# Wider spacing of a ring of weight tiles in a 1-core transformer trunk

## Chip, cores and metric

The kernel runs on one core of one Trainium2 chip. The metric is the time of one execution on the device, in microseconds (us). Before the change it is 2625.57 us, the median of three runs from 2624.16 to 2627.06 us.

## What is computed

Two layers, each a token mixer and a gated feed-forward network, over 1024 tokens of 1024 features in float32. Layer 0 mixes with forgetting attention (8 heads of 128), layer 1 with chunked retention (4 heads, chunks of 64 tokens). Cut to what matters:

```python
def rmsnorm(x, g):
    return x * rsqrt(mean(x * x, -1) + 1e-6) * g

def forgetting_attention(h, w_in, b_f, w_out):        # w_in: 1024 x (3*1024 + 8)
    q, k, v, f = split(h @ w_in)
    c = cumsum(log_sigmoid(f + b_f), axis=1)          # one decay per token and head
    s = q @ k.T * 128 ** -0.5 + (c[query] - c[key])   # causal
    return softmax(s) @ v @ w_out

def retention(h, w_in, w_out):                        # w_in: 1024 x 6144
    q, k, v, g = split(h @ w_in); q, k = rotate(q), rotate(k) / 16
    # per chunk: inner products with decay, a state carried from chunk to chunk
    return (silu(g) * normalised(y)) @ w_out          # w_out: 2048 x 1024

def swiglu(h, w_in, w_out):                           # 2816 hidden features
    gu = h @ w_in
    return (silu(gu[:2816]) * gu[2816:]) @ w_out

x = x + forgetting_attention(rmsnorm(x)); x = x + swiglu(rmsnorm(x))
x = x + retention(rmsnorm(x));            x = x + swiglu(rmsnorm(x))
out = rmsnorm(x)
```

## The kernel before

Activations stay in feature-major tiles of 128 partitions by 512 tokens. Every operand of a product is an exact sum of two float32r parts, a high part and a low part. `split` (L97 to L99) makes them: ScalarE casts the source into the high tile (L98), VectorE subtracts it from the source into the low tile (L99). A product of two such operands takes three matmuls: high by high, high weight by low activation, low weight by high activation (L106 to L108 in `mm_u`, L638 to L640 in `Products`). Each matmul loads its own 128x128 block of weights and streams 512 columns of activations past it.

The large products of the feed-forward and the retention projections are Strassen-Winograd products in 2 x 2 blocks, seven in place of eight. `Blocks` loads a pair of weight tiles into `st`, forms their sums on VectorE (`s1`, `s2`) and splits each on demand; `Products` runs 12 matmuls for each of the seven: four 128-column slices of one split weight tile, three matmuls a slice. A few products (`pair_N`, L737 to L739, and `v_pair`, L256 to L258) use the split weight tile as the streamed operand in place of the loaded one.

All split weights go through one ring, made in `wh_wl` (L79 and L80) from the pool `wp`: six tiles with tag `wh` for high parts and six with tag `wl` for low parts. A tile holds 512 float32r values per partition and 16 spare ones, 2112 bytes in all. The split activations are tiles with tag `b` of exactly 2048 bytes, in the pools `bpa` (ahead of the ring in memory) and, after the attention stage, `bpb` (behind it).

In the built program the first `wh` slot starts at byte 107008 of each partition (a multiple of 256) and the slots follow at the pitch of 2112 bytes; the six `wl` slots come right behind them, from byte 119680. So the starting byte, modulo 256, is 0, 64, 128, 192, 0, 64 for the six `wh` slots and 128, 192, 0, 64, 128, 192 for the six `wl` slots. The four slices of a tile lie 512 bytes apart and have the tile's own residue. All `b` tiles start at multiples of 256. A slot is given to the tile that asks next when its last reader is done, so high and low slots come in all pairings.

In the attention stage (a pool `fox` that is released before the Strassen stages) `attend` (L313) ends each block of 512 queries with the reciprocal of the denominator in a tile `rec` and the block's output in a tile `o`, one buffer each (L379 to L398): two ScalarE activations (L383, L384) and two VectorE instructions (L385, L386) make the reciprocal, L387 multiplies it into `o`, and `split` reads `o`. `decay_bias` (L269) keeps its 128x64 intermediates in small tiles; `f_s` is read last at L289 and `f_lf` is written at L292.

The order of the instructions on each engine comes from the framework's scheduler.

Of the kernel before, what the change touches and what calls it, by code (L numbers as in the profile page):

```python
# [17 lines left out]
P = 128  # L18
# [19 lines left out]
def trunk(ctx, tc, nc, d, out):  # L38
# [22 lines left out]

# [1 line left out]
    bpa = ctx.enter_context(tc.tile_pool(name="bpa", bufs=32))  # L63
# [15 lines left out]
    def wh_wl(width=512):  # L79
        return [wp.tile([P, 512 + 16], F32R, tag=t, name=nm(t))[:, :width] for t in ("wh", "wl")]  # L80

# [29 lines left out]

# [1 line left out]
    class Norm:  # L113
# [69 lines left out]

    # =================== forgetting attention ===================
    with ExitStack() as fs:
# [6 lines left out]
        def half(tag, bufs=2):  # L192
            if tag in ("t", "x"):
                return yp.tile([P, H], F32, tag="y", name=nm(tag))
            return fp.tile([P, H], F32, tag=tag, name=nm(tag), bufs={"rec": 1, "o": 1}.get(tag, bufs))

# [72 lines left out]
        def decay_bias(z):  # L269
            n = TB * FOX_HEADS  # L270
            zz = z.rearrange("p b h -> p (b h)")
            m = small([P, n], "f_m", 1)
            sg = small([P, n], "f_sg", 1)
            s = small([P, n], "f_s", 1)
            s2 = small([P, n], "f_s2", 1)
            a = small([P, n], "f_a", 1)
            nc.vector.tensor_scalar(m, zz, -1.0, None, op0=ALU.mult)
            nc.vector.tensor_tensor(m, m, zz, op=ALU.min)
            sig = nc.scalar.activation(sg, m, AF.Sigmoid)
            with tc.issue_after(sig.ins):  # L280
                nc.scalar.preload_act_table_set("natural_log_exp_and_others")
            nc.vector.tensor_scalar(s2, sg, -1.0, 2.0, op0=ALU.mult, op1=ALU.add)
            nc.vector.reciprocal(s2, s2)
            nc.vector.tensor_tensor(s, sg, s2, op=ALU.mult)
            nc.vector.tensor_tensor(s2, s, s, op=ALU.mult)
            nc.vector.tensor_scalar(a, s2, 1.0 / 19.0, None, op0=ALU.mult)
            for j in range(8, 0, -1):
                nc.vector.scalar_tensor_tensor(a, a, 1.0 / (2 * j + 1), s2, op0=ALU.add, op1=ALU.mult)
            nc.vector.scalar_tensor_tensor(a, a, 1.0, s, op0=ALU.add, op1=ALU.mult)  # L289
            nc.vector.tensor_scalar(m, zz, 0.0, None, op0=ALU.min)  # L290
            lf = small([P, n], "f_lf", 1)
            nc.vector.scalar_tensor_tensor(lf, a, -2.0, m, op0=ALU.mult, op1=ALU.add)  # L292
            ps = mp.tile([P, H], F32, tag="ms", name=nm("c"))
            nc.tensor.matmul(ps[:, 0:n], tri, lf, start=True, stop=True)
            nc.tensor.matmul(ps[:, n:2 * n], ones, lf, start=True, stop=True)
            pre = small([P, TB + 1, FOX_HEADS], "f_pre", 1)
            nc.vector.memset(pre[:, 0, :], 0.0)
            for b in range(TB):
                nc.vector.tensor_tensor(pre[:, b + 1, :], pre[:, b, :],
                                        ps[:, n + b * FOX_HEADS:n + (b + 1) * FOX_HEADS], op=ALU.add)  # L300
            c = small([P, TB, FOX_HEADS], "f_c", 1)
            nc.vector.tensor_tensor(c, ps[:, 0:n].rearrange("p (b h) -> p b h", b=TB), pre[:, 0:TB, :], op=ALU.add)
            dk = []
            for qh in range(2):
                t = small([P, TB, FOX_HEADS], f"f_d{qh}", 1)
                nc.vector.tensor_tensor(t, pre[:, 4 * qh + 2:4 * qh + 3, :].to_broadcast([P, TB, FOX_HEADS]), c,
                                        op=ALU.subtract)
                dk.append(t)
            return dk
# [3 lines left out]
        def attend(h, kk, qq, vs, dk, rks):  # L313
# [4 lines left out]
            def weights(qb):  # L318
# [57 lines left out]
                else:  # L376
                    den = mp.tile([P, H], F32, tag="ms", name=nm("den"))
                    nc.tensor.matmul(den, ones, acc, start=True, stop=True)
                rec, o = half("rec"), half("o")  # L379
                n = 2 if h == FOX_HEADS - 1 and qb else 1  # L380
                for cs in (slice(i * H // n, (i + 1) * H // n) for i in range(n)):
# [4 lines left out]
                    nc.vector.scalar_tensor_tensor(r, sm[:, cs], 2.0, r, op0=ALU.subtract, op1=ALU.mult)  # L386
                    nc.vector.scalar_tensor_tensor(o[:, cs], pv[:, cs], -1.0, r, op0=ALU.mult, op1=ALU.mult)  # L387
                if h >= FOX_HEADS - 2:
# [4 lines left out]
                    for cs in (slice(i * H // n, (i + 1) * H // n) for i in range(n)):  # L393
                        split(hi[:, cs], lo[:, cs], o[:, cs])
                    return
                oh = fp.tile([P, H], F32R, tag="ph", name=nm("oh"), bufs=3)
                ol = fp.tile([P, H], F32R, tag="pl", name=nm("ol"), bufs=3)
                split(oh, ol, o)  # L398
                nc.sync.dma_start(od[h][0][:, HALF[qb]], oh.bitcast(F32))
# [15 lines left out]
        reloads = []  # L415
        # the keys of the first two heads, a pass over the features as they come
        ks, pss = [], {}
# [27 lines left out]
        for h in range(FOX_HEADS):  # L445
# [6 lines left out]
            if h == FOX_HEADS - 1:  # L452
# [1 line left out]
                wo, ops = [], {}  # L454
# [7 lines left out]

        # the tiles so far with all heads but the last; the first of them leave the banks
        part = {}
# [15 lines left out]

    # =================== Strassen-Winograd products ===================
    # C = A B with A = W^T in 2 x 2 blocks (two column tiles, even and odd k tiles) and
    # B in 2 x 2 blocks (even and odd k tiles, two token halves): seven products.
    bpb = ctx.enter_context(tc.tile_pool(name="bpb", bufs=24))
# [10 lines left out]

    # where the sums of a phase are kept
    NAMES = ("B11", "T2", "T1", "T3", "B21", "B22", "T4")
# [40 lines left out]
    class Stored:  # L538
        """The sums of a group of four pairs of feature tiles, kept in memory, split at their first use."""

# [28 lines left out]
    class Blocks:  # L569
        """The four blocks of a pair of column tiles and their sums, split on demand."""  # L570

# [46 lines left out]
    class Products:  # L618
        """The seven products of one pair of 128-column tiles, feature-major."""

# [21 lines left out]
    def pair_acc(src, X, y, first):  # L642
        """Adds the products of one pair to the sums y over the groups of feature tiles."""
        prod = Products(src, X)
# [25 lines left out]
    def paired_out(wsrc, stored, scale_rows, xold):  # L670
        """x + (scaled) act @ W over the groups of eight feature tiles whose sums are in memory."""
        ys = [{} for _ in range(4)]
# [20 lines left out]
    def pair_T(src, X):  # L693
        """Feature-major C11, C12, C21, C22 of one pair of 128-column tiles."""
        prod = Products(src, X)
# [20 lines left out]
    def pair_N(srcs, X):  # L716
        """Token-major C11, C12, C21, C22 of one pair of 256-column tiles, as two tiles of two token blocks."""
        ws = [Blocks(s) for s in srcs]
# [58 lines left out]
    def load_units(pool, src, gate=None):  # L777
        """A feature tile over all tokens from memory, split in two, by token halves."""
        r = []
# [10 lines left out]
    def out_proj(wsrc, y, acts, xnew, gi, nextw, pools):  # L790
        """y + act @ W: returns the operands of the next phase and its norm."""
        norm = Norm(gi, sp, "sc", "sacc", 4)
# [17 lines left out]

    # =================== SwiGLU ===================
    def ffn(i, X, nrm, xold, xnew, last, nw, pools):
# [60 lines left out]

# [1 line left out]
    norm = Norm(1, sp, "sc", "sacc", 4)  # L875
# [34 lines left out]

    # =================== retention ===================
    qd = [[dp.tile([P, S], F32, tag=f"qd{k}", name=f"qd{k}") for k in range(2 * h, 2 * h + 2)] for h in range(RET_HEADS)]
# [81 lines left out]
    def load_k(h):  # L994
        """Keys by feature, split, and the first half of them times kappa by token, split."""
        ks, kf = [], []
# [23 lines left out]
    def state(kt, vv):  # L1020
        """Sum over the first half of the tokens of key times value, by key feature."""
        r = []
# [146 lines left out]
def _alt(w, i):  # L1169
    """Every other column tile."""  # L1170
    k, n = w.shape
    return w.reshape(k, n // 256, 2, P)[:, :, i].reshape(k, n // 2)


def _quad(u, v, js):
    """A pair of column tiles as four blocks: the first over even and over odd k tiles, then the second."""
    r = [w.reshape(KT // 2, 2, P, -1)[list(js)].transpose(2, 1, 0, 3).reshape(P, 2, -1) for w in (u, v)]
# [76 lines left out]
```

## Time and profile before

| | |
|---|---|
| time, median of three runs | 2625.57 us |
| span of the profiled execution | 2626.0 us |
| TensorE (PE) busy | 2600.0 us, 99% |
| weight loads (PEld) busy | 2179.9 us, 83% |
| VectorE (DVE) busy | 1960.2 us, 75% |
| ScalarE (ACT) busy | 1155.9 us, 44% |
| GpSimd (POOL) busy | 167.6 us, 6% |
| granted TensorE clock, mean | 0.998 of full speed |

The profile gives the profiled execution's own time as this span, from its first to its last instruction. Matmuls overlap in the pipeline, so the duration of one (394 ns) is longer than the distance from its start to the start of the next; what the stream costs is that distance, called the pitch below. A window of the profile that holds N matmuls without a break in T us has a pitch of T/N.

### The profile page before, as it was taken

The numbers are of one execution on the slowest core, as the hardware profiler recorded it, in microseconds if no ns is written. First come the engines' busy times: TensorE is split into PE (matmuls) and PEld (weight loads), VectorE is DVE, ScalarE is ACT, GpSimd is POOL, SyncE is SP. The second block draws the span as 40 slices with busy tenths as digits, with TensorE's granted clock in tenths as the row PEclk, the third lists the DMA queues.
The fourth block names the chain that finished last, engine by engine and source line by source line (L and its number), as shares of the span: only waits on it lengthen the run. The fifth ranks groups of instructions, "written<-read, shape, count | busy, mean of one in ns | idle before, by whom it ended". The sixth has DMA issues, their size and how long they took to land.

```text
span 2626.0 us, 35148 instructions
## 1 busy us (share of the span) xinstructions
PE 2600.0 (99%) x12808; PEld 2179.9 (83%) x12808; DVE 1960.2 (75%) x3367; ACT 1155.9 (44%) x2168; POOL 167.6 (6%) x147
## 2 busy tenths in 40 slices
PE   9999999999999999999999999999999999999998
PEld 8878887888888878889898989898888888887888
DVE  6798888877767778987667676885567776768795
ACT  6566666533233444453333425662353233335533
POOL 0143322000000000001000010000000000000000
PEclk9999999999999999999999999999999999999999
DMA  3111143332332345533332325655522332325441
GB/s 129 44 57 65 49 145 119 122 106 95 109 104 97 109 152 180 167 107 117 104 113 96 113 101 160 189 196 192 190 85 85 104 111 86 109 84 183 156 158 65
DMA packets 137694, 312.11 MB, mean 119 GB/s; under 512 B 15665, under 2 KB 28721, under 8 KB 137521
## 3 DMA queue, kind: packets, MB, share of 16 engines
q1 hardware_dynamic: 136800, 309.33, 35.1%
q8 instruction: 100, 1.64, 0.3%
q14 instruction: 74, 0.60, 0.1%
q10 hardware_dynamic: 720, 0.55, 0.1%
HBM read 217.54 MB, written 92.27 MB: 118 GB/s over the span
## 4 chain that ended last, share of the span: by engine, by line
PE 89%; DMA 4%; DVE 3%; issue 2%; ACT 1%; POOL 0%; SPq 0%; DVEq 0%; POOLq 0%; ACTq 0%
PE mm L638 17%; PE mm L640 17%; PE mm L639 17%; PE mm L106 7%; PE mm L107 7%; PE mm L108 7%; PE mm L738 2%; PE mm L739 2%; PE mm L737 2%; DMA st<-vd 1%; DMA st<-ac_T 1%; PE mm L256 1%; PE mm L258 1%; PE mm L257 1%; DVE b L99 1%
## 5 line engine op out<-in xcount | busy, mean ns | idle before, releaser
L639 PE MATMUL mm<-b,wh 128*128 128x512 f32 x2128 | 836.8, 394 | 0.0
L638 PE MATMUL mm<-b,wh 128*128 128x512 f32 x2128 | 832.9, 395 | 3.2 <-ACT 22_4397_22190 L653 1.8
L640 PE MATMUL mm<-b,wl 128*128 128x512 f32 x2128 | 819.5, 394 | 0.1
L98 ACT CAST wh<-st 128x512 fp32r<-128x512 f32 (+1 forms) x449 | 275.2, 616 | 578.4 <-PE mm L639 409.4
L638 PEld LDWEIGHTS mm<-b,wh 128*128 128x128 f32 x2128 | 400.3, 188 | 97.8 <-ACT 22_4397_22190 L653 2.2
L640 PEld LDWEIGHTS mm<-b,wl 128*128 128x128 f32 x2128 | 399.8, 188 | 94.1 <-DVE wl L99 0.9
L639 PEld LDWEIGHTS mm<-b,wh 128*128 128x128 f32 x2128 | 400.0, 188 | 91.9 <-DVE b L99 0.2
L99 DVE TENSOR_TENSOR wl<-st,wh 128x512 fp32r<-128x512 f32 (+1 forms) x449 | 311.5, 697 | 55.8 <-ACT wh L98 51.8
L98 ACT CAST wh<-s 128x512 fp32r<-128x512 f32 x252 | 156.0, 621 | 413.3 <-PE mm L639 356.8
L106 PE MATMUL mm<-b,wh 128*128 128x512 f32 x736 | 289.7, 397 | 8.4 <-ACT b L126 5.7
L107 PE MATMUL mm<-b,wh 128*128 128x512 f32 x736 | 290.0, 395 | 1.4 <-DVE b L99 1.4
L108 PE MATMUL mm<-b,wl 128*128 128x512 f32 x736 | 289.9, 395 | 0.0
L99 DVE TENSOR_TENSOR wl<-s,wh 128x512 fp32r<-128x512 f32 x252 | 182.6, 727 | 41.4 <-ACT wh L98 39.7
L106 PEld LDWEIGHTS mm<-b,wh 128*128 128x128 f32 x736 | 138.9, 189 | 40.5 <-ACT b L126 6.5
L107 PEld LDWEIGHTS mm<-b,wh 128*128 128x128 f32 x736 | 138.8, 189 | 32.0 <-DVE b L99 1.8
L108 PEld LDWEIGHTS mm<-b,wl 128*128 128x128 f32 x736 | 138.7, 188 | 31.5
L98 ACT CAST b<-st 128x512 fp32r<-128x512 f32 (+1 forms) x216 | 125.1, 612 | 81.7 <-DMA st<-ac_T 30.0
L99 DVE TENSOR_TENSOR b<-st,b 128x512 fp32r<-128x512 f32 (+1 forms) x216 | 140.0, 674 | 27.9 <-ACT b L98 22.5
L711 DVE TENSOR_TENSOR u<-mm,u 128x512 f32<-128x512 f32 x60 | 41.4, 689 | 116.1 <-PE mm L640 115.9
L738 PE MATMUL mm<-wl,b 128*128 128x256 f32 x448 | 126.0, 281 | 0.0
L739 PE MATMUL mm<-wh,b 128*128 128x256 f32 x448 | 125.9, 281 | 0.0
L737 PE MATMUL mm<-wh,b 128*128 128x256 f32 x448 | 125.8, 281 | 0.0
(514 smaller groups left out, 3965.2 us busy)
## 6 DMA issues: line engine op xcount, KB each, us to landing
st<-ffn_in SPq DMA_DIRECT2D x88, 512.0 KB, 3.5
st<-ffn_out_pairs SPq DMA_DIRECT2D x32, 512.0 KB, 5.4
st<-ac_T SPq DMA_DIRECT2D x32, 512.0 KB, 4.6
ac_T<-t SPq DMA_DIRECT2D x48, 256.0 KB, 2.4
st<-ac_B SPq DMA_DIRECT2D x24, 512.0 KB, 4.6
st<-fox_qk SPq DMA_DIRECT2D x32, 256.0 KB, 2.7
xo<-xd SPq DMA_DIRECT2D x32, 256.0 KB, 3.1
ac_B<-p SPq DMA_DIRECT2D x32, 256.0 KB, 3.1
```

The source lines that it names most:

```text
L98: nc.scalar.copy(hi, src)
L99: return nc.vector.tensor_tensor(lo, src, hi.bitcast(F32), op=ALU.subtract)
L106: nc.tensor.matmul(ps, wh, xh, start=(first and k == 0), stop=False)
L107: nc.tensor.matmul(ps, wh, xl, start=False, stop=False)
L108: nc.tensor.matmul(ps, wl, xh, start=False, stop=(last and k == n - 1))
L638: nc.tensor.matmul(ps, hi[:, js], th, start=f, stop=False, skip_group_check=not new)
L639: nc.tensor.matmul(ps, hi[:, js], tl, start=False, stop=False, skip_group_check=not new)
L640: nc.tensor.matmul(ps, lo[:, js], th, start=False, stop=(j == 3), skip_group_check=not new)
L711: nc.vector.tensor_tensor(u2, banks["c"], u2, op=ALU.add)
L737: nc.tensor.matmul(o, th[:, tk], hi[:, js], start=f, stop=False, skip_group_check=sk)
L738: nc.tensor.matmul(o, th[:, tk], lo[:, js], start=False, stop=False, skip_group_check=sk)
L739: nc.tensor.matmul(o, tl[:, tk], hi[:, js], start=False, stop=(j == 3), skip_group_check=sk)
```

## The change

Each tile of the ring gets 64 spare values in place of 16: 2304 bytes in place of 2112. Twelve tiles of 192 bytes more are 2304 bytes per partition. They come from two tiles of the attention stage that go: `o` (2048 bytes), whose value is now written over `rec`, and `f_lf` (256 bytes), which becomes a second use of `f_s`.

```diff
     def wh_wl(width=512):
-        return [wp.tile([P, 512 + 16], F32R, tag=t, name=nm(t))[:, :width] for t in ("wh", "wl")]
+        return [wp.tile([P, 512 + 64], F32R, tag=t, name=nm(t))[:, :width] for t in ("wh", "wl")]
...
-            return fp.tile([P, H], F32, tag=tag, name=nm(tag), bufs={"rec": 1, "o": 1}.get(tag, bufs))
+            return fp.tile([P, H], F32, tag=tag, name=nm(tag), bufs={"rec": 1}.get(tag, bufs))
...
-            lf = small([P, n], "f_lf", 1)
+            lf = small([P, n], "f_s", 1)
...
-                rec, o = half("rec"), half("o")
+                rec = half("rec")
...
-                    nc.vector.scalar_tensor_tensor(o[:, cs], pv[:, cs], -1.0, r, op0=ALU.mult, op1=ALU.mult)
+                    nc.vector.scalar_tensor_tensor(r, pv[:, cs], -1.0, r, op0=ALU.mult, op1=ALU.mult)
...
-                        split(hi[:, cs], lo[:, cs], o[:, cs])
+                        split(hi[:, cs], lo[:, cs], rec[:, cs])
...
-                split(oh, ol, o)
+                split(oh, ol, rec)
```

The other lines of the diff only remove comments. Apart from the new names, the instructions of every engine stand in the same order in the built program as before. Three ScalarE instructions have another list of waits: the first activation of L383 in two of the 16 blocks of queries now also waits for VectorE (the last reader of the shared tile in the block before), and one cast of L98 no longer does.

In the built program the `wh` slots start at byte 107008 as before and follow at 2304 bytes, the `wl` slots start at byte 120832. 2304 is nine times 256, so all twelve start at multiples of 256, alternately at 0 and 256 modulo 512. What lies behind the ring moves up by 2304 bytes or, behind a removed tile, by less; every one of the `b` tiles still starts at a multiple of 256.

## Rows read from the trace of the kernel before

**Rows 1.** Page, part 1: busy us (share of the span) and instructions, by engine.

```profile
PE 2600.0 (99%) x12808; PEld 2179.9 (83%) x12808; DVE 1960.2 (75%) x3367; ACT 1155.9 (44%) x2168; POOL 167.6 (6%) x147
```

**Rows 2.** Windows of two feed-forward stages: busy us and (instructions) by engine, clock, DMA.

```profile
530.00:925.00 395.00, 395.00 (x1706) 320.42 (x1705) 284.98 (x459) 130.57 (x222) 0.00 (x0) 1.00 0.31 107
2100.00:2365.00 265.00, 265.00 (x1146) 215.18 (x1145) 187.11 (x302) 82.07 (x139) 0.00 (x0) 1.00 0.29 97
```

**Rows 3.** Page, part 5, matmul groups: shapes, count | busy, mean ns | idle before.

```profile
L639 PE MATMUL mm<-b,wh 128*128 128x512 f32 x2128 | 836.8, 394 | 0.0
...
L107 PE MATMUL mm<-b,wh 128*128 128x512 f32 x736 | 290.0, 395 | 1.4 <-DVE b L99 1.4
...
L738 PE MATMUL mm<-wl,b 128*128 128x256 f32 x448 | 126.0, 281 | 0.0
```

**Rows 4.** Waits of ScalarE and of weight loads: who, for whom: us, times, longest.

```profile
ACT wh L98 <- PE mm L639: 766.2, 395, 4.6
...
PEld mm L638 <- ACT wh L98: 1.9, 4, 0.8
...
PEld mm L640 <- DVE wl L99: 0.9, 2, 0.5
```

**Rows 5.** Timeline, TensorE, 652 to 661 us: start, length, instruction; 11 rows between each.

```profile
652.10 0.40 PE L638 MATMUL mm<-b,wh 128*128 128x512 f32 x1
...
654.88 0.40 PE L638 MATMUL mm<-b,wh 128*128 128x512 f32 x1
...
657.68 0.39 PE L638 MATMUL mm<-b,wh 128*128 128x512 f32 x1
...
660.40 0.40 PE L638 MATMUL mm<-b,wh 128*128 128x512 f32 x1
```

**Rows 6.** The same timeline, three later products of 12 matmuls: first start, next product's start.

```profile
754.66 0.40 PE L638 MATMUL mm<-b,wh 128*128 128x512 f32 x1
...
757.42 0.39 PE L638 MATMUL mm<-b,wh 128*128 128x512 f32 x1
...
768.49 0.39 PE L638 MATMUL mm<-b,wh 128*128 128x512 f32 x1
...
771.28 0.40 PE L638 MATMUL mm<-b,wh 128*128 128x512 f32 x1
...
1413.71 0.39 PE L638 MATMUL mm<-b,wh 128*128 128x512 f32 x1
...
1416.43 0.39 PE L638 MATMUL mm<-b,wh 128*128 128x512 f32 x1
```

**Rows 7.** The same timeline near the end, weights in tiles `b`; 93 matmuls between.

```profile
2555.99 0.39 PE L106 MATMUL mm<-b,b 128*128 128x512 f32 x1
...
2577.30 0.39 PE L106 MATMUL mm<-b,b 128*128 128x512 f32 x1
```

**Rows 8.** Windows in which VectorE is nearly always busy; columns as in rows 2.

```profile
2500.00:2520.00 20.00, 20.00 (x88) 16.19 (x87) 19.93 (x34) 4.35 (x7) 0.00 (x0) 1.00 0.36 119
2520.00:2540.00 20.00, 20.00 (x88) 16.21 (x87) 20.00 (x35) 11.68 (x20) 0.00 (x0) 1.00 0.48 158
...
1020.00:1040.00 20.00, 19.84 (x87) 15.80 (x86) 20.00 (x35) 4.15 (x7) 0.00 (x0) 1.00 0.24 80
1040.00:1060.00 20.00, 20.00 (x88) 16.16 (x87) 19.97 (x35) 7.16 (x12) 0.00 (x0) 1.00 0.40 132
```

**Rows 9.** Timelines of VectorE and ScalarE at the attention's closest pair of blocks, then groups.

```profile
396.92 0.68 DVE L99 TENSOR_TENSOR b<-o,b 128x512 fp32r<-128x512 f32 x1
...
397.61 0.63 ACT L383 ACTIVATE rec<-M 128x512 f32<-128x512 f32 x1 [0.53 <-POOL M L374]
...
L99 DVE TENSOR_TENSOR ol<-o,oh 128x512 fp32r<-128x512 f32 x12 | 8.4, 696 | 3.2 <-ACT oh L98 3.1
...
L98 ACT CAST oh<-o 128x512 fp32r<-128x512 f32 x12 | 7.4, 619 | 9.0 <-DVE o L387 9.0
```

## Prediction

> **What bounds the kernel now.** I read the page's first part, then windows of long stages, the matmul groups, the waits, and last the timeline of single matmuls. TensorE is busy for 2600.0 of 2626.0 us; VectorE is next with 1960.2 [rows 1]. So the time is the number of matmuls times their pitch, plus some 26 us at the start, in the attention, at stage borders and at the end. In two long feed-forward stages nothing interrupts the stream: 1706 matmuls in 395.00 us and 1146 in 265.00 us, a pitch of 231.5 and 231.2 ns (one or two of each count reach over an edge) [rows 2]. The weights are no bottleneck in supply: the ScalarE cast that fills a `wh` slot waited 766.2 us for TensorE's matmul L639 to free one, while weight loads waited 1.9 us for a cast and 0.9 us for a low part [rows 4]. What remains to be moved is the pitch itself.
>
> The pitch isn't the same everywhere, and it goes with the slot of the ring. Rows 5 cut out three products of 12 matmuls in a row, same engine, same shapes, no wait between them. The first has its high weights in the slot at 117568 (residue 64 modulo 256) and its low ones at 119680 (128): 2.78 us, 231.7 ns each. The second has 113344 (192) and 126016 (64): 2.80 us, 233.3 ns. The third has 115456 and 123904, both multiples of 256: 2.72 us, 226.7 ns. The slots come from the program, the times from the rows. I looked at every product of 12 in one tile pair: seven have both tiles on a multiple of 256. The first is the third of rows 5, the slowest starts at 754.66 us (2.76 us, 230.0 ns), the last at 1413.71 (2.72 us, 226.7 ns) [rows 6]; the mean of the seven is 227.6 ns. No other pairing of residues is that fast; 128 with 128, for one, takes 2.79 us at 768.49 us, 232.5 ns [rows 6]. The streamed operand is a `b` tile on a multiple of 256 in all of them. A second witness has nothing of the ring: near the end both operands are `b` tiles, and 94 matmuls take 21.31 us, 226.7 ns [rows 7].
>
> **The pitch of the ring.** After the change all twelve slots are multiples of 256, which the seven products of ring tiles and the `b` tiles of rows 7 show already. Matmuls of 512 columns with weights in the ring: three groups of 2128 and three of 736 [rows 3], 8592 in all. Each goes from 231.5 ns [rows 2] to 227.6: 3.9 ns, and 8592 x 3.9 ns = 33.5 us. The bounds: if every one ran as in rows 7, 4.8 ns and 41.2 us; if as in the slowest of the seven, 230.0 ns, 1.5 ns and 12.9 us. I take the mean because the slow one of the seven is entered from a tile off the multiple, and after the change no ring tile is.
>
> Where the ring's tile is streamed and not loaded (L737 to L739, three groups of 448 with 256 columns [rows 3], and the L256 to L258 groups), no row singles out a residue. The bound upward is the same 3.9 ns each, 1344 x 3.9 ns = 5.2 us; below, a loss as large. I take nothing, since half the columns pass and the loaded operand there is a `b` tile already on a multiple. The attention's own products (`kh`, `qh`, `vh`, `ph`) keep their residues modulo 256 but not modulo 512; no row separates them; 8 heads by 12 key tiles by six matmuls (L328 to L330, L362 to L364) are 576, at 3.9 ns either way 2.2 us. I take nothing.
>
> **What gives some back.** A shorter pitch needs its inputs 1.7% sooner. Casts run far ahead [rows 4], so supply holds. But in some 60 us from 2500 and 40 us from 1020 VectorE is busy for 19.9 to 20.0 of 20 us [rows 8]; if it set the pace there, those 100 us would not shrink: 100 us x 1.7% = 1.7 us lost. I count that in full. Below, the slots filled ahead may cover it (0).
>
> **The shared tiles.** With `o` on top of `rec`, the first activation of L383 of the next block has to wait until the last `split` read the old value: the cast (619 ns) and the subtraction (696 ns), 1.3 us longer than before [rows 9]. The closest pair of blocks shows the margin: the subtraction starts at 396.92 us and takes 0.68, and the next L383 starts at 397.61, 0.01 us later [rows 9]; it was waiting for GpSimd. It is one of the two blocks with an added wait; all others lie further apart. So it costs nothing as things stand. If that cover goes, L384 and the attention's casts and exponentials queue behind L383 on ScalarE, and TensorE waits for the casts: 0 to 1.3 us for this block, and 16 x 1.3 = 21 us if every block paid on TensorE's path. I take 0. Writing over `rec` (L387) and over `f_s` (L292) reads and writes on VectorE in its own order: no wait, no added instruction, 0.
>
> **Sum.** 2626.0 (the span) - 33.5 + 1.7 = 2594.2 us. The span is 0.4 us above the median of the runs, so 2594 us.
>
> **The rivals.** (a) *Half is given back.* The pitch shortens, but the transitions between tiles keep part of the loss, or VectorE sets the pace in more places than rows 8. From half of the forecast's 31.8 us (15.9) down to the slowest of the seven (12.9): 2610 to 2613 us, say 2611. For it: one of seven is at 230.0 ns. Against: six are not, and TensorE hardly waits anywhere.
>
> (b) *The start address has no effect.* Then the seven products are fast for another reason, such as what other engines did then, and nothing changes: 2625.6 us, 2620 to 2631. Against it: the neighbours in rows 5 follow each other within 9 us in one stage. For it stands a rule. The Trainium skill ("SBUF — State Buffer", Who interferes with whom) gives TensorE two independent read ports, one for the streamed operand and one for weight loads, and says that it never waits on anyone; its section Operand start alignment asks only for a multiple of the element size. By these the start of a slot can't matter and the sum is 2625.6 us. Rows 5 speak against that: 233.3 ns and 226.7 ns back to back, with the slots' residues as what differs.
>
> (c) *All on one residue collide: slower.* Mechanism: the weight load and the stream then begin on the same residue every time, in the inner loop L638 to L640, and the mixed residues of now spread them. Price: equal residues off the multiple show 232.5 ns (128 with 128 [rows 6]), the worst pairing 233.3 [rows 5], so 8592 x 1.0 to 1.8 ns = 8.6 to 15.5 us, 2634 to 2641 us. It decides as soon as products with all operands on multiples of 256 pass 231.5 ns. Rows 5 to 7 hold just such products, and they are the fastest.
>
> (d) *The shared tile stalls every block*: + 21 us, which with the shorter pitch is 2615 us and without it 2646. Rows 9 leave no sign of it; I put it in with (a) and (c).
>
> **How the numbers follow.** Forecast, 2583 to 2604 us: 0.68. (a), 2604 to 2618: 0.18. (b): 0.08. (c), with the part of (d) that ends above: 0.06. A measurement of this kernel tells about 0.2%, 5.3 us, from no change, so the forecast and (a) are both faster: 0.86; same 0.08; slower 0.06. The range: below the 2583 us that 41.2 us and some of the 5.2 us give, little is left out; above, it takes in most of (a), to 2614 us. That holds the forecast's 0.66 and some 0.14 of (a).
>
> **What would show it.** Right: a pitch near 227.6 ns in the stages of rows 2 (the same 1706 matmuls in some 388 us), hardly a product of 12 over 2.76 us, DVE's and ACT's work per instruction as before, an attention stage of the same length up to 1 us. The give-back shows as PE idle around 2460 to 2540 us. Wrong: a pitch still at 231 in these stages (b), or above it (c), or L383 waiting for L99 with TensorE idle behind it (d). What would make the sum wrong first is the mean of seven products standing for 8592 matmuls: they come from two `wh` slots and one `wl` slot (107008, 115456 and 123904: 0, 256 and 0 modulo 512).

## The result and the profile after

The changed kernel takes 2594.3 us (median of four runs, 2593.46 to 2598.24), the kernel before 2625.6 us. The ratio is 0.9885, with a 95% interval from 0.9871 to 0.9899: 31.3 us or 1.15% faster. The profiled execution is the slowest of the four (2598.24 us); its span is 2596.5 us.

The page of the changed kernel, its span, the busy time by engine and four matmul groups (columns as in [rows 1] and [rows 3]):

```profile
span 2596.5 us, 35149 instructions
...
PE 2568.1 (99%) x12808; PEld 2182.1 (84%) x12808; DVE 1960.0 (75%) x3367; ACT 1157.3 (45%) x2168; POOL 167.5 (6%) x147
...
L639 PE MATMUL mm<-b,wh 128*128 128x512 f32 x2128 | 828.6, 390 | 0.0
...
L107 PE MATMUL mm<-b,wh 128*128 128x512 f32 x736 | 287.7, 392 | 1.6 <-DVE b L99 1.6
...
L738 PE MATMUL mm<-wl,b 128*128 128x256 f32 x448 | 126.8, 283 | 0.0
```

TensorE is as full as before and does the same 12808 matmuls in 31.9 us less busy time; VectorE works for the same time as before [rows 1]. The 512-column groups are 3 to 4 ns shorter per instruction, the 256-column group that streams the ring is 2 ns longer [rows 3]. A window inside the first feed-forward stage of the changed kernel (us, then busy us and instructions of PE, PEld, DVE, ACT, POOL, clock, DMA share, GB/s):

```profile
560.00:900.00 340.00, 340.00 (x1501) 281.53 (x1501) 244.35 (x394) 110.02 (x186) 0.00 (x0) 1.00 0.30 101
```

1501 matmuls, one or two of them over an edge, are 226.5 ns each by this window (226.7 from start to start), where [rows 2] have 231.5. And in the timeline there is no longer a fast and a slow product. The first matmuls of three slices in a row in the changed kernel, two rows left out between each (start us, length, instruction):

```profile
600.18 0.39 PE L638 MATMUL mm<-b,wh 128*128 128x512 f32 x1
...
600.86 0.39 PE L638 MATMUL mm<-b,wh 128*128 128x512 f32 x1
...
601.54 0.39 PE L638 MATMUL mm<-b,wh 128*128 128x512 f32 x1
```

Three matmuls take 0.68 us, 226.7 ns each, as in the one fast product of [rows 5] and at the end of the program [rows 7].

Where the time went, in the two profiled executions. The pitches below are means of the distances from one matmul's start to the next over the whole trace, pauses left out; the last row sums what distances exceed the usual of their width by, where that is over 15 ns.

| part | matmuls | before, ns | after, ns | us |
|---|---|---|---|---|
| 512 columns, weights in the ring | 8592 | 231.70 | 227.06 | -39.9 |
| 256 columns, ring tile streamed, retention values | 1344 | 118.33 | 119.95 | +2.2 |
| 256 and 264 columns, ring tile streamed, attention values | 768 | 118.8 | 120.0 | +0.9 |
| the attention's own products | 576 | | | +0.4 |
| waits and what follows them | | 30.5 us | 37.3 us | +6.8 |

Together -29.6 us; the spans differ by 29.5. The 31.3 us are the difference of the medians, and no run at the median was profiled.

Most of the last line comes from a single place. Waits of TensorE in the changed kernel (who, for whom: us, times, longest), then its timeline at that wait, then windows ahead of it, in it and behind it (columns as above):

```profile
PE mm L638 <- ACT 22_1722_8770 L653: 3.5, 1, 3.5
```

```profile
923.64 0.39 PE L640 MATMUL mm<-b,wl 128*128 128x512 f32 x1
927.52 0.79 PE L638 MATMUL mm<-b,wh 128*128 128x512 f32 x1 [3.50 <-ACT 22_1722_8770 L653]
```

```profile
920.00:923.50 3.50, 3.50 (x17) 2.90 (x16) 3.50 (x7) 1.58 (x3) 0.00 (x0) 1.00 0.71 167
923.90:927.50 3.60, 0.12 (x1) 0.00 (x0) 1.94 (x4) 1.65 (x4) 0.00 (x0) 0.79 0.96 378
927.50:930.00 2.50, 2.48 (x6) 2.00 (x7) 2.50 (x5) 1.56 (x3) 0.00 (x0) 0.50 0.95 367
930.00:932.60 2.60, 2.60 (x8) 2.02 (x7) 2.60 (x6) 0.00 (x0) 0.00 (x0) 0.50 0.55 197
932.70:936.00 3.30, 3.30 (x15) 2.66 (x15) 1.88 (x4) 2.51 (x5) 0.00 (x0) 0.98 0.21 79
```

The first output product of the feed-forward waits for a bank that ScalarE copies out at L653, and ScalarE stands behind two casts whose source, a sum reloaded from memory (`ac_T`), lands late: its timeline just ahead of L653 shows the wait.

```profile
925.85 1.14 ACT L98 CAST b<-st 128x512 fp32r<-128x512 f32 x2 [3.69 <-DMA st<-ac_T]
926.89 0.58 ACT L653 COPY 22_1722_8770<-mm 128x512 f32<-128x512 f32 x1
```

After 3.5 us without a matmul the granted clock is 0.50, which is the 1.2 GHz level, and the 12 matmuls that follow take until 932.81 us, 0.44 us each in place of 0.23; from then on the clock is back. So the pause costs 3.7 us and its echo 12 x 0.21 = 2.5 us. In the kernel before the same wait was 0.9 us long, and the clock stayed at 1.00; its wait and the window around it:

```profile
PE mm L638 <- ACT 22_1738_8786 L653: 0.9, 1, 0.9
```

```profile
936.50:938.00 1.50, 1.46 (x6) 1.24 (x7) 1.50 (x4) 1.50 (x3) 0.00 (x0) 1.00 0.85 307
```

### The profile page after: what moved, and what is told of

Read it like the earlier page. It is cut to its first block, busy times and chain, and to the rows that moved or that the text cites. A ratio compares the mean times of both kernels' runs of the same rounds, so it can differ in the third digit from the quotient of the medians.

```text
span 2596.5 us, 35149 instructions
## 1 busy us (share of the span) xinstructions
PE 2568.1 (99%) x12808; PEld 2182.1 (84%) x12808; DVE 1960.0 (75%) x3367; ACT 1157.3 (45%) x2168; POOL 167.5 (6%) x147
## 4 chain that ended last, share of the span: by engine, by line
PE 88%; DMA 4%; DVE 3%; ACT 2%; issue 2%; POOL 0%; SPq 0%; DVEq 0%; POOLq 0%; ACTq 0%
PE mm L638 16%; PE mm L639 16%; PE mm L640 16%; PE mm L106 7%; PE mm L107 7%; PE mm L108 7%; PE mm L738 2%; PE mm L739 2%; PE mm L737 2%; DMA st<-ac_T 2%; DVE b L99 1%; PE mm L256 1%; PE mm L257 1%; PE mm L258 1%; DMA st<-ac_B 1%
## 5 line engine op out<-in xcount | busy, mean ns | idle before, releaser
L638 PE MATMUL mm<-b,wh 128*128 128x512 f32 x2128 | 824.6, 391 | 6.9 <-ACT 22_1722_8770 L653 3.5
L639 PE MATMUL mm<-b,wh 128*128 128x512 f32 x2128 | 828.6, 390 | 0.0
L640 PE MATMUL mm<-b,wl 128*128 128x512 f32 x2128 | 809.7, 390 | 0.3 <-DVE wl L99 0.3
L98 ACT CAST wh<-st 128x512 fp32r<-128x512 f32 (+1 forms) x449 | 275.2, 617 | 561.2 <-PE mm L639 395.7
L638 PEld LDWEIGHTS mm<-b,wh 128*128 128x128 f32 x2128 | 400.0, 188 | 94.2 <-ACT wh L98 4.7
L639 PEld LDWEIGHTS mm<-b,wh 128*128 128x128 f32 x2128 | 400.2, 188 | 82.5 <-DVE b L99 0.7
L98 ACT CAST wh<-s 128x512 fp32r<-128x512 f32 x252 | 156.2, 621 | 400.0 <-PE mm L639 343.6
L108 PE MATMUL mm<-b,wl 128*128 128x512 f32 x736 | 287.2, 391 | 0.0
L99 DVE TENSOR_TENSOR wl<-s,wh 128x512 fp32r<-128x512 f32 x252 | 183.4, 730 | 38.9 <-ACT wh L98 36.2
L107 PEld LDWEIGHTS mm<-b,wh 128*128 128x128 f32 x736 | 138.8, 189 | 29.6 <-DVE b L99 2.1
L98 ACT CAST b<-st 128x512 fp32r<-128x512 f32 (+1 forms) x216 | 125.2, 612 | 82.2 <-DMA st<-ac_T 31.2
```

The source lines that it names most:

```text
L98: nc.scalar.copy(hi, src)
L99: return nc.vector.tensor_tensor(lo, src, hi.bitcast(F32), op=ALU.subtract)
L107: nc.tensor.matmul(ps, wh, xl, start=False, stop=False)
L108: nc.tensor.matmul(ps, wl, xh, start=False, stop=(last and k == n - 1))
L638: nc.tensor.matmul(ps, hi[:, js], th, start=f, stop=False, skip_group_check=not new)
L639: nc.tensor.matmul(ps, hi[:, js], tl, start=False, stop=False, skip_group_check=not new)
```

## The experiments

The theory at the outset: matmuls with weights in the ring are slow because its tiles start off a multiple of 256 bytes. Rivals: the sharing of tiles does it, the wider pitch as such, or one common residue. All ratios are to the kernel before, with a 95% interval where there is one.

**Sharing alone.** The ring stays at 2112 bytes.

```diff
-        return [wp.tile([P, 512 + 64], F32R, tag=t, name=nm(t))[:, :width] for t in ("wh", "wl")]
+        return [wp.tile([P, 512 + 16], F32R, tag=t, name=nm(t))[:, :width] for t in ("wh", "wl")]
```

> The two shared tiles of the attention stage alone, the ring at 2112 bytes as before. Theory (the starts of the ring's tiles make the gain, sharing costs nothing): 2625 to 2627 us, the pitch in the window of 1706 matmuls again 231.5 ns. Rival (sharing, or what it moves behind the ring, brings a part of the gain or hides a cost): 2610 us or less, or 2635 or more.

2626.3 us, ratio 1.0001 (0.9991 to 1.0010). The window from 560 to 900 us holds 1469 matmuls, a pitch of 231.4 ns (231.6 from start to start):

```profile
560.00:900.00 340.00, 340.00 (x1469) 275.84 (x1469) 239.23 (x385) 105.44 (x177) 0.00 (x0) 1.00 0.28 97
```

Sharing neither gains nor costs.

**A pitch of 2176 bytes.** Starts at 0 and 128 in turn (`512 + 32`).

> A pitch of 2176 bytes: the tiles start at 0 and 128 modulo 256 in turn, so half of them off the multiple of 256. Theory (256 is what counts): products of 12 with both tiles on 0 at 227 ns, 0 with 128, 128 with 0 and 128 with 128 at 231.5 to 233 ns as in the kernel before; in all a pitch of some 231 ns, 2615 to 2623 us. Rival (a multiple of 128 is enough, or any pitch over 2112): 2594 to 2600 us.

2624.3 us, ratio 0.9996 (0.9987 to 1.0006). By the starts in the timeline, some 2770 matmuls with their own and the next tile at 0 take 227.9 ns, some 2980 with both at 128 take 233.1, and the crossings, slow both ways, 233.0 and 233.7. So multiples of 128 are not enough, and a wider pitch isn't what helps. Both kinds are a little slower than foreseen, and the time comes out just above the 2615 to 2623 us that were expected; a gain isn't shown, since the interval holds 1.

**All ring tiles 64 bytes in.** The pitch of 2304 stays, nothing else moves.

```diff
-        return [wp.tile([P, 512 + 64], F32R, tag=t, name=nm(t))[:, :width] for t in ("wh", "wl")]
+        return [wp.tile([P, 512 + 64], F32R, tag=t, name=nm(t))[:, 16:16 + width] for t in ("wh", "wl")]
```

> The changed kernel with every ring tile's contents 64 bytes in, so that all twelve start at 64 modulo 256 while all else stays where it is. Theory (a loaded tile has to start on a multiple of 256): a pitch of 233 ns in the feed-forward stages, 8592 x 6 ns = 52 us over the changed kernel, 2640 to 2648 us. Rival (one common residue, or the wider pitch itself, is enough): 2594 us.

2637.5 us, ratio 1.0046 (1.0030 to 1.0063): 43 us over the changed kernel, 12 us over the kernel before, and just under the 2640 to 2648 us that were expected. The 512-column pitch is 233.3 ns from start to start; the window, with 1459 matmuls in 340 us, gives 233.0:

```profile
560.00:900.00 340.00, 340.00 (x1459) 273.95 (x1458) 237.90 (x383) 103.28 (x174) 0.00 (x0) 1.00 0.29 99
```

One common residue isn't enough, and a wide pitch at the wrong start is worse than the mixture.

**Everything 64 bytes further.** A tile of 64 bytes ahead of all others, so that the ring and the `b` tiles start at 64 alike.

```diff
     cp = ctx.enter_context(tc.tile_pool(name="cp", bufs=1))
+    shift = cp.tile([P, 16], F32, tag="shift", name="shift")
+    nc.gpsimd.memset(shift, 0.0)
```

> The changed kernel with a tile of 64 bytes ahead of everything, so that ring tiles and streamed tiles all start at 64 modulo 256, equal to each other. If the start itself has to be a multiple of 256: 233 ns as with the ring alone at 64, and the products of b with b slow too, 2640 us or more. If only the distance of the loaded from the streamed tile counts: 227 ns, 2592 to 2597 us.

2598.0 us, ratio 0.9895 (0.9880 to 0.9909), and over all 8592 matmuls a pitch of 227.08 ns from start to start. The window, with 1502 matmuls:

```profile
560.00:900.00 340.00, 340.00 (x1502) 281.53 (x1501) 243.82 (x392) 110.13 (x185) 0.00 (x0) 1.00 0.30 101
```

The time is 1 us over what the distance gave and far from the 2640 us of the first theory. Here that theory falls: with every ring tile at 64, off the multiple of 256, the pitch is that of the changed kernel. What counts is not the start itself but the distance from the start of the streamed tile to that of the loaded one, modulo 256. The `b` tiles have been at 0 all along, which is why the two couldn't be told apart in the trace of before. The next weight load runs during a matmul's stream (in the changed kernel one for L639 starts at 922.51 us, the matmul of L638 at 922.50); whether the distance to a matmul's own tile or to the next one's counts isn't separated, as nearly all tiles start alike in these kernels.

**Other distances.** The ring tiles 16 bytes and 192 bytes in (`4:4 + width` and `48:48 + width`), with the changed kernel otherwise.

> The changed kernel with the ring tiles' contents 16 bytes in, so a distance of 16 between the starts of loaded and streamed tiles, modulo 256. If the distance has to be a multiple of 256: over 230 ns for the 512-column matmuls with weights in the ring and 2615 us or more. If only distances of 64 and more hurt: 227 ns, 2594 to 2598 us.

2628.7 us, ratio 1.0004 (0.9993 to 1.0015), 231.6 ns. Sixteen bytes lose what the change gains. But 231.6 is a mean of two paces: with the same starts throughout, this one execution runs at 233.3 ns from start to start in the first of these two windows and at 226.7 ns, the pace of the changed kernel, in the second:

```profile
600.00:700.00 100.00, 100.00 (x430) 81.00 (x429) 69.92 (x114) 30.41 (x51) 0.00 (x0) 1.00 0.30 103
1800.00:1900.00 100.00, 100.00 (x443) 82.81 (x442) 53.05 (x77) 29.70 (x50) 0.00 (x0) 1.00 0.57 194
```

The ten runs of this kernel lie between 2617.6 and 2630.0 us, where the four at 64 bytes lie within 1.3 us. That the runs differ in how long they keep either pace would fit this; only one was profiled.

> The same with 192 bytes in. In the kernel before, products with both tiles at 192 against streamed tiles at 0 took some 229.5 ns a matmul. Distance theory, by these: 229.5 ns, 2612 to 2620 us, between the changed kernel and the one at 64 (233.3 ns, 2637 us). Rival (any distance but 0 costs alike): 233 ns, 2637 us.

2600.9 us, ratio 0.9906 (0.9893 to 0.9920), 229.06 ns for the 512-column matmuls. The expectation of 2612 to 2620 us was missed. By 8592 x 2.0 ns the time would be 17 us over the changed kernel; it is 6.6. The 256-column matmuls that stream the ring give most of the rest back: they take 113.5 ns in place of 119.95, 8.7 us over 1344. Windows inside the first head's values, in the changed kernel and in this one:

```profile
1210.00:1225.00 15.00, 15.00 (x127) 15.00 (x127) 8.37 (x14) 5.38 (x17) 0.00 (x0) 1.00 0.41 133
```

```profile
1212.00:1227.00 15.00, 15.00 (x135) 15.00 (x134) 8.83 (x14) 5.97 (x18) 0.13 (x1) 1.00 0.42 136
```

**A map of distances.** One profile in which the distance goes up by 16 bytes from one input product of the feed-forward to the next, then some smaller ones.

```diff
-            c11, c12, c21, c22, t = pair_T(nw if f == 0 and nw else d["ffn_in"][i, f], X)
+            c11, c12, c21, c22, t = pair_T(nw if f == 0 and nw else Blocks(d["ffn_in"][i, f], 4 * f if f < 16 else (1, 2, 3, 6, 50, 62)[f - 16]), X)
...
-        cc = pair_N((d["ret_v"][2 * h], d["ret_v"][2 * h + 1]), X)
+        cc = pair_N((d["ret_v"][2 * h], d["ret_v"][2 * h + 1]), X, (8, 24, 32, 40)[h])
```

(`Blocks`, `pair_N` and `wh_wl` take the distance in values of 4 bytes and pass it on.)

> A map in one profile: the changed kernel with another distance in each of the first 16 input products of both feed-forward stages (0, 16, 32 to 240 bytes), then 4, 8, 12, 24, 200 and 248 bytes; for the streamed ring tiles 32, 96, 128 and 160 bytes in the four heads of the retention values. Distance theory: 227 ns at 0, and by the runs so far 231.6 to 232.5 at 16, 233 at 64 and 128, 229 at 192, with what lies between unknown; if the start counts by whole 16-byte pieces only, 4, 8 and 12 bytes stay at 227. Streamed tiles: 120 ns at 0, 117.8 at 64, 113.5 at 192. Rival (the loss is one step, alike at every distance but 0): 233 ns everywhere else.

Mean distance of starts, 512 columns, own and next tile at the same distance; 4862 matmuls at 0, 149 to 160 at each other:

| bytes | 0 | 4 | 8 | 12 | 16 | 24 | 32 | 48 | 64 | 80 | 96 |
|---|---|---|---|---|---|---|---|---|---|---|---|
| ns | 227.3 | 232.5 | 230.8 | 232.0 | 228.8 | 231.1 | 233.1 | 233.3 | 233.2 | 231.8 | 234.2 |

| bytes | 112 | 128 | 144 | 160 | 176 | 192 | 200 | 208 | 224 | 240 | 248 |
|---|---|---|---|---|---|---|---|---|---|---|---|
| ns | 233.3 | 233.0 | 233.2 | 233.4 | 230.0 | 231.1 | 230.7 | 232.9 | 233.2 | 227.4 | 233.4 |

Only 240 bytes come near 0; 4 bytes are enough to lose 5 ns, so whole 16-byte pieces are not what counts. The streamed ring tiles took 116.7, 120.0, 120.0 and 118.7 ns at 32, 96, 128 and 160 bytes. This kernel was run once and took 2609.0 us. At 16 and at 192 bytes it differs from the two kernels that have one distance throughout (231.6 and 229.1 ns there): away from 0, the distance alone doesn't fix the pitch. The single distances show how. At each the pitches repeat a short pattern, the same in both layers, and some distances have more than one: at 192 bytes the means of 20 matmuls in a row go from 233.3 to 228.9 ns within one input product, at 16 bytes they lie between 226.7 and 233.6. So the table holds means over some 150 matmuls, and not a fixed price of each distance.

**Streams and attention.** The ring at 0 where it is loaded, 64 bytes in where it is streamed, and the attention's `kh` and `qh` at one residue, by a 288-byte tile that moves to another pool.

```diff
-                hi, lo = wload(src[:, k * wid:(k + 2) * wid], 2 * wid)
+                hi, lo = wload(src[:, k * wid:(k + 2) * wid], 2 * wid, 16)
...
-            pre = small([P, TB + 1, FOX_HEADS], "f_pre", 1)
+            pre = small([P, TB + 1, FOX_HEADS], "pre", 1)
...
-        ws = [Blocks(s) for s in srcs]
+        ws = [Blocks(s, 16) for s in srcs]
```

> The changed kernel, with the ring tiles that are streamed against b tiles (the retention values and the attention values, 256 and 264 columns) 64 bytes in, and with a 288-byte tile moved out of the attention's pool so that its loaded and streamed tiles start at one distance of 0 modulo 256. If the distance theory holds for both: 119.9 to 117.8 ns for 1344 matmuls (2.9 us) and about 1 us for the attention values, and 233 to 227 ns for 288 matmuls of the attention (1.7 us): some 5 us under the changed kernel, 2588 to 2592 us. If the 256-column streams were faster at 64 bytes for another reason, 2593 us or more.

2591.7 us, ratio 0.9872 (0.9858 to 0.9885). The 1344 streamed matmuls take 117.8 ns, as foreseen; the attention's own 512-column products go from 233.3 to 231.3 ns, not to 227. In the attention they alternate with matmuls on ring weights whose two tiles both start 128 bytes away from theirs (32 and 160 modulo 256), which may be why; that wasn't separated.

> The changed kernel once more on the same chip, to compare with the runs of this call: 2592 to 2598 us. Its stalls beyond the pitch tell whether the 3.7 us wait for a reloaded sum of the feed-forward (at 924 us in its profile) is part of the change or of one run: under 2 us there if it is of one run.

The changed kernel again: 2593.7 us (2590.9 to 2600.6), ratio 0.9890 (0.9875 to 0.9905), with a profiled span of 2589.2 us and the same 227.06 ns. Its waits beyond the pitch sum to 30.2 us, against 30.5 in the kernel before and 37.3 in the first profile of the change: the 3.5 us wait isn't there. The spans of the two profiles differ by 7.3 us, most of it this wait with its echo. The runs of the changed kernel spread from 2590.9 to 2600.6 us; whether the others differ by the same wait isn't shown.

**Streams at 192.** Only the streamed ring tiles, 48 values in (`wload(..., 48)` and `Blocks(s, 48)`).

> The changed kernel, with only the ring tiles that are streamed against b tiles (attention and retention values) 192 bytes in. By the run with all ring tiles at 192: 119.95 to 113.5 ns for 1344 matmuls, 8.7 us, and as much each for the 768 of the attention values, 4.9 us; together 13.6 us under the changed kernel, 2580 to 2583 us, if VectorE keeps up in the retention values; 2585 to 2590 if it or the loads set the pace there. The 512-column matmuls stay at 227 ns.

2589.9 us, ratio 0.9858 (0.9842 to 0.9875): the fastest here, though its interval touches that of the changed kernel. The attention values take 116.6 ns (120.0 in the changed kernel), but the retention values 117.8 and not 113.5:

```profile
1205.00:1220.00 15.00, 15.00 (x130) 15.00 (x129) 7.83 (x13) 5.68 (x17) 0.00 (x0) 1.00 0.43 139
```

The program gives each of these 1344 matmuls the same start for both operands in this kernel as in the one with all tiles 192 bytes in.

**Both once more**, to see if an execution picks its pace or the kernel does.

> The kernel with all ring tiles 192 bytes in, profiled once more. In its first profile the 1344 streamed 256-column matmuls ran at 113.5 ns, in the kernel that moves only the streamed tiles by 192 bytes at 117.8 ns with the same starts of every operand. If the pitch off the distance of 0 is set by the kernel: 113.5 and 229.0 ns again. If an execution settles into one of several paces: another value here, such as 117.8, at the same addresses.

2598.5 us (one run); 113.49 ns and 229.06 ns, as in its first profile. In both profiles the first 16 of the 1344 swing between 113 and 123 ns and the rest settle at 113 to 114.

> The kernel with only the streamed ring tiles 192 bytes in, profiled once more. If the kernel sets the pace: 117.8 ns again for the 1344 streamed matmuls and 114.9 for those of the attention values, and 227.0 ns for the 8592. If an execution does: 113.5 ns or another value for the first, while those at a distance of 0 stay at 227.0 ns.

2591.1 us (one run); 117.78 ns and 227.05 ns, as in its first profile. So each of these two kernels kept its pace from one profile to the next, and with equal starts in these matmuls they differ by 4.3 ns. Here, as at 16 bytes, the same starts carry more than one pace. What decides between them is open; the matmuls that run ahead of the stage have other starts in the two kernels, and that they decide it wasn't tested.

## Why the prediction was right

2594 us were forecast and 2594.3 measured. The mechanism and the main term were right; that the sum came out to 0.3 us is luck, since a gain that was too small and losses that were too small cancel.

- *What bounds the kernel, and the seven products.* Right. The pitch is what moved, and a few products of 12 in the trace of before told the pitch of 8592 matmuls. By the starts that the program gives there are twelve of them and not seven, the last at 1969.17 us, with a mean of 227.7 ns; that changes the forecast by less than 1 us. The term was a little too small: the mean of the seven was 227.6 ns, and the entry from other tiles slowed it, as the prediction said of the slowest; the measured 227.06 lies between it and the 226.7 of [rows 5] and [rows 7]. The pitch of before was taken as 231.5 from [rows 2]; the trace's mean is 231.70. So 33.5 us were forecast and 39.9 gained.
- *The ring tile as the streamed operand*, taken as nothing with 5.2 us either way: a loss of 3.1 us for both places. The bound held, the value was off; the kernel at 64 bytes shows that it is the start of these tiles, 117.8 against 119.95 ns.
- *The attention's products*, taken as nothing: +0.4 us.
- *What gives some back.* 1.7 us where VectorE is always busy. Wrong place. In the changed kernel VectorE is as full in these stretches as in [rows 8], and TensorE isn't held up (the matmuls that took 39.9 us from 1020 us on before take 38.9):

```profile
2470.00:2490.00 20.00, 20.00 (x89) 16.52 (x88) 19.93 (x34) 4.36 (x7) 0.00 (x0) 1.00 0.35 118
2490.00:2510.00 20.00, 20.00 (x90) 16.56 (x89) 20.00 (x35) 11.01 (x19) 0.00 (x0) 1.00 0.49 160
```

  What came back in the profiled run is 6.8 us, most of it at the reloaded sums at 924 us, and in the second profile nothing. The step that failed is the choice of the place: the sum looked for the loss where an engine is full, and the largest came at a stage border where a load landed late in one of the two profiles.
- *The shared tiles.* Right: ratio 1.0001 alone. The closest pair of blocks in [rows 9] did lose its cover, once: ScalarE waited 0.9 us for VectorE at L383. TensorE did not pay for it there: its one wait for L387, the instruction that makes the output of a block, is 0.9 us before and after.

```profile
  DVE b L99: 0.9, 1
```

- *Rival (b) and the rule behind it.* The start address does have an effect. The Trainium skill ("SBUF — State Buffer", Who interferes with whom) says that TensorE's two read ports are independent and that it never waits on anyone. The prediction took that to mean that the start of a slot can't matter. Here a shift of one of the two operands by 64 bytes costs 6.2 ns a matmul and a shift of both costs nothing; the measurement decides. What makes the two operands depend on each other no run shows.
- *Rival (c)*, a collision when all start on one residue, is the opposite of what the runs show: for 512 columns equal starts are the fast case, at 0 and at 64. Its price took 128 with 128 for all equal residues off the multiple; 192 with 192 took only some 229.5 ns in the trace of before.
- *The mechanism as the prediction put it*, a multiple of 256, was right for this kernel and wrong in general: at 64 the start is as fast as at 0, if the streamed operand starts there too. The text had noticed that the streams all begin at 0 and didn't make a rival of it.

## What to carry to other kernels

When TensorE is 99% busy, look at the distance from one matmul's start to the next and sort it by the buffers of the two operands: here a few buffers that happened to be well placed told what all would do. A padded pitch that isn't a multiple of 256 bytes spreads the starts over the residues; here making loaded and streamed tiles start alike was worth 1.15%, for 2304 bytes. That holds for matmuls of 512 columns; those of 256 columns lost a little by it. And a pause at a stage border can cost more than itself: one of 3.7 us was followed by a stretch at the lower clock that cost 2.5 us more.

## What the runs showed of the hardware

- The pitch of 512-column matmuls that load 128x128 weights depends on the distance of the two operands' starts modulo 256: 227.06 ns at 0 (with both at 0 or both at 64), and on average 228.8 to 234.2 at nearly all others, with 4 bytes enough and 240 bytes an exception at 227.4.
- Off 0 the same starts can carry more than one pace: with 16 bytes 226.7 and 233.3 ns in two stages of one execution, with 192 bytes 228.9 and 233.3 within one input product of the map.
- For 256 columns with the ring streamed equal starts are not the fast case: 119.95 ns at 0 and 120.0 at 96 and 128 bytes, 117.8 at 64, 116.7 at 32, and 113.5 or 117.8 at 192, the values at 0 and 192 the same again in a second profile of each kernel. Why is open, and so is what decides between two paces.
- After 3.5 us without a matmul the granted clock was 0.50, at the 1.2 GHz level, for the next 5 us; after 0.9 us, in the kernel before, it stayed at 1.00.
